# Two placements of exponentials on ScalarE in a hybrid decoder step: behind which high part of the weights they run

## The chip, the core and the metric

The kernel runs on one core of one Trainium2 chip. The metric is device time in microseconds (us) from start to end of one execution; the figure given for a kernel is the median of several runs. A profile is one further execution, recorded by the hardware profiler, with times in us from the start of its span.

The core's engines are TensorE (PE: matmuls; PEld: its weight loads), VectorE (DVE), ScalarE (ACT), GpSimd (POOL) and SyncE (SP, which here only issues DMAs). Each takes its instructions in the order that the program gave it.

## The reference

The reference is one inference step of a hybrid decoder layer, for 256 prompt tokens and 8 sample tokens (264 columns). One combined input projection gives queries, keys and values of a windowed attention, and z, x, B, C and dt of a state-space mixer. The mixer's scan over the prompt, which the change touches, works in two chunks of 128 tokens:

```python
la = jnp.cumsum(dt * a, axis=2)
seg = la[:, :, :, None] - la[:, :, None, :]
decay = jnp.exp(jnp.where(causal, seg, -jnp.inf))
cb = jnp.einsum('bclgn,bcsgn->bclsg', cm, bm)
y = jnp.einsum('bclsgh,bcsghp->bclghp', cb[..., None] * decay, xdt)
...
y = y + jnp.einsum('bclgn,bcghpn->bclghp', cm, h_prev) * jnp.exp(la)[..., None]
```

The exponential in `decay` is that of the differences inside a chunk; `jnp.exp(la)` in the last line is that of the decays by which the state carried from the chunk before enters the output. After the mixer come an output projection, a cross-attention over 256 memory tokens and a convolutional feed-forward block, all in float32.

## The kernel before

**Projections.** Every weight matrix is streamed from HBM in parts of 128 x 1024 floats (512 KB). `weights` (lines 76 to 92) loads a part into wraw (line 83, queue of SP, four buffers), ScalarE casts it to a high part whi (line 89), and VectorE subtracts to get the low part wlo (line 90); both have four buffers. The list `highs` collects the casts and `lows` the subtractions in the order in which the program writes them down. `proj` multiplies each part three times (high by high, high by low, low by high: lines 105 to 107), 264 columns at a time. In the input projection a pair of output blocks (256 columns) takes two units of two parts, so four parts: four casts, four subtractions, 96 matmuls. The pair's two sums lie in two PSUM banks; VectorE evacuates them, with the row factor r0, into u (line 789 for x, B and C; line 948 for z). The banks of the tag "mm" are three and of "t" two, so the second half of a pair can need a bank that the pair before has to give up.

**The mixer's order.** x comes in four groups of two pairs each (`conv_group`, lines 932 to 940: projection, causal convolution on ScalarE line 770 and VectorE line 772, tanh line 773, and the sample tokens' part with tsm, line 782), then z in eight pairs (`z_pair`, line 946 on; tanh line 953, squares 293 and 296, splits 98). The scan of group g (`ssd_prompt`, lines 832 to 897) is written down between them: group 0 behind the projections of conversion group 1, group 1 behind those of group 2, groups 2 and 3 behind the first and the second z pair.

**The scan of one group.** `logs` (line 820 on) loads the tile late with rows of la, broadcast over partitions: two blocks of 1024 columns, one per chunk (line 825), and 512 columns for the carried state (line 829, two DMAs). It is issued on SP's queue behind the last weight load written down by then, from the second call on. ScalarE then turns each chunk's block into decays: eight Relus that subtract la (line 847) and an exponential (line 848). VectorE multiplies by the masked product of B and C (line 849), TensorE multiplies by x (line 877). The 512 columns get one exponential (line 890); VectorE multiplies the carried state's output by it (line 891), and GpSimd adds it to x (line 892).

**What sets the order.** A planner in the compiler simulates the program and writes each engine's instructions in the order in which the simulation could start them, those marked with `high_priority` (all of `weights`) first. `tc.issue_after(ins)` adds one condition for the instructions in its block that run on ins's engine: they come behind ins there. Line 845 puts a chunk's Relus and exponential behind `highs[2 * c - 4]`: of the four casts of the last pair written down, the first for chunk 0 and the third for chunk 1. Line 890 has no such condition. Nearby there is also the attention of the sample tokens, whose matmuls (line 739) read zz, which VectorE fills (line 732) from a transposition (line 284), and the product of the sample tokens' states (lines 929 and 930).

Of the kernel before, what the change touches and what calls it, by code (L numbers as in the profile page):

```python
# [9 lines left out]
AF = mybir.ActivationFunctionType  # L10
# [38 lines left out]
def hybrid_decoder_step_kernel(ctx: ExitStack, tc: tile.TileContext, I, O):  # L49
    nc = tc.nc  # L50
    V, S, P, PE = nc.vector, nc.scalar, nc.gpsimd, nc.tensor
# [9 lines left out]
    def psum(tag):  # L61
        return ps.tile([128, 512], F32, tag=tag, name=tag, bufs=banks[tag])
# [39 lines left out]
    lows, highs = [], []  # L102
# [166 lines left out]
    def pc(name, i=0, n=1):  # L269
        o = _PC[name][0]  # L270
        return par[:, o + i:o + i + n]
# [10 lines left out]
    def tr(out, in_):  # L282
        k = in_.shape[0]
        return PE.transpose(out, in_, cst[0:k, C_ID:C_ID + k])  # L284
# [547 lines left out]
    def ssd_prompt(g):  # L832
        hs = slice(8 * g, 8 * g + 8)
        hp = mp.tile([128, 512], F32, tag="hp", name="hp", bufs=1)
        late = lates[g]
        p = psum("s")
        es, xdts = [], []
        for c in range(2):
            cs = slice(c * 128, c * 128 + 128)
            cbt = p[:, 256 * c:256 * c + 128]  # L840
            cbm = p[:, 256 * c + 128:256 * c + 256]
            PE.matmul(cbt, BT[:, g, cs], CT[:, g, cs], start=True, stop=True)
            V.tensor_tensor(out=cbm, in0=cbt, in1=tri, op=ALU.mult)
            e = late[:, 1024 * c:1024 * c + 1024].rearrange("p (h l) -> p h l", h=8)
            with tc.issue_after(highs[2 * c - 4].ins):
                for j in range(8):
                    S.activation(out=e[:, j, :], in_=e[:, j, :], func=AF.Relu, scale=-1.0, bias=la[:, c * 32 + 8 * g + j:c * 32 + 8 * g + j + 1])
                S.activation(out=e, in_=e, func=AF.Exp, scale=-1.0)
            V.tensor_tensor(out=e, in0=e, in1=cbm.unsqueeze(1).broadcast_to([128, 8, 128]), op=ALU.mult)
            es.append(e)  # L850
        sts = []
        for c in range(2):
            p = psum("x")
            for i in range(4):
                tr(p[:, i * 128:i * 128 + 128], xs[g][:, i, c * 128:c * 128 + 128])
            xdt = mp.tile([128, 8, 64], F32, tag="xdt", name="xdt", bufs=2)
            V.tensor_tensor(out=xdt, in0=p.rearrange("p (h q) -> p h q", h=8),
                            in1=dtn[:, c, hs].unsqueeze(2).broadcast_to([128, 8, 64]), op=ALU.mult)
            xdts.append(xdt)
            xw = mp.tile([128, 8, 64], F32, tag="bc", name="xw", bufs=2)  # L860
            V.tensor_tensor(out=xw, in0=p.rearrange("p (h q) -> p h q", h=8),
                            in1=de[:, c, hs].unsqueeze(2).broadcast_to([128, 8, 64]), op=ALU.mult)
            sts.append(xw)

        def state(c):
            st = psum("x")
            PE.matmul(st, Bn[:, c, g, :], sts[c].rearrange("p h q -> p (h q)"), start=True, stop=True)  # L867
            return st

        S.copy(out=hp, in_=state(0))  # L870
        for i in range(4):
            S.activation(out=xs[g][:, i, :TP], in_=xs[g][:, i, :TP], func=AF.Copy, scale=pc("d_skip", 4 * g + i))
        ys = [psum(k) for k in ("y", "s")]

        def own(c, h):
            o = (h % 2) * 64
            return PE.matmul(ys[c][o:o + 64, (h // 2) * 128:(h // 2) * 128 + 128], xdts[c][:, h, :], es[c][:, h, :], start=True, stop=True)

        with tc.issue_after(own(1, 7).ins):
            for c in range(2):  # L880
                for h in range(7 if c else 8):
                    own(c, h)
        for c in range(2):
            x = xs[g][:, :, c * 128:c * 128 + 128]
            V.tensor_tensor(out=x, in0=x, in1=ys[c].rearrange("p (i l) -> p i l", i=4), op=ALU.add)
        yi = psum("y")
        for i in range(4):
            PE.matmul(yi[:, i * 128:i * 128 + 128], hp[:, i * 128:i * 128 + 128], CT[:, g, 128:256], start=True, stop=True)
        ti = late[:, 2048:2560].rearrange("p (i l) -> p i l", i=4)
        S.activation(out=ti, in_=ti, func=AF.Exp)  # L890
        V.tensor_tensor(out=ti, in0=yi.rearrange("p (i l) -> p i l", i=4), in1=ti, op=ALU.mult)
        P.tensor_tensor(out=x, in0=x, in1=ti, op=ALU.add)
        st = state(1)
        hl = hp.rearrange("p (h q) -> p h q", h=8)
        P.tensor_tensor(out=hl, in0=hl, in1=d1[:, hs].unsqueeze(2).broadcast_to([128, 8, 64]), op=ALU.mult)
        V.tensor_tensor(out=hp, in0=hp, in1=st, op=ALU.add)
        nc.sync.dma_start(out=O["state_p"][g], in_=hp)
# [91 lines left out]
    with tc.issue_after(marks["load"].ins):  # L989
        logs()  # L990
    ssd_prompt(0)
    conv_group(2)
    with tc.issue_after(marks["load"].ins):
        logs()
    ssd_prompt(1)
    conv_group(3)
    with tc.issue_after(marks["load"].ins):
        logs()
    nc.sync.dma_start(out=O["conv_new"], in_=cnew)
    for i in range(8):  # L1000
        z_pair(i)
        ssd_sample(*([3, 1] if i in (1, 3, 5) else [1]))
        if i < 2:
            ssd_prompt(2 + i)
        if i in (3, 5, 7):
            res_load()
# [646 lines left out]
```

## Time and profile before

| | before |
|---|---|
| runs, us | 1385.97, 1385.55, 1385.59; median 1385.59 |
| profiled execution, us | 1385.11 |
| its span, us | 1383.3 |
| mean granted TensorE clock | 0.999 |
| DMA | 298.31 MB, mean 216 GB/s |

In a page of the profile a row of engines gives busy time, share of the span and instructions. In a list in order of time, a row has its start, its duration, engine, line and operation, what it writes and reads ("whi<-wraw"), shapes, and in square brackets the idle time of the engine before it with what ended it. In a list of waits, a row names who waited for whom, the total in us, how often, and the longest. A tile's view gives smallest, median and largest duration in ns and the starts of the first and the last instruction. The label "SPq" stands for DMAs issued on SP's queue. The profiler sees some of ScalarE's and VectorE's instructions overlap by about 0.1 us.

### The profile page before, as it was taken

The page shows a single profiled execution, that of the slowest core. Times are in us where ns is not written, and L with a number is a line of the kernel's source. Part 1 is how long each engine was busy: PE and PEld are TensorE (multiplying, and loading weights), DVE is VectorE, ACT ScalarE, POOL GpSimd, SP SyncE. Part 2 cuts the span into 40 slices and gives each one's busy share as a digit, 9 for nine tenths or more (in the row PEclk, how much of TensorE's full clock was granted, in tenths as well). Part 3 has the DMA queues.
Part 4 walks back from the last instruction along what each step waited for, and adds up shares of the span by engine and source line. Part 5 has one row for each costly group of instructions (what it writes and reads, how often), then busy time and mean ns, then how long its engine had stood idle before and what let it go on. Part 6 is the DMA issues. An engine that isn't in the chain of part 4 may idle for free.

```text
span 1383.3 us, 28658 instructions
## 1 busy us (share of the span) xinstructions
PE 1372.1 (99%) x11412; PEld 1348.4 (97%) x11412; DVE 1042.0 (75%) x1797; ACT 770.8 (56%) x1255; POOL 90.6 (7%) x284
## 2 busy tenths in 40 slices
PE   9999989999999999999999999999999999999998
PEld 8999989999999999899999999999999999999998
DVE  8879869999997784579777775776577657765655
ACT  7667666755545555566565544554455445543532
POOL 0000101111100000002010000000000000000000
PEclk9999999999999999999999999999999999999999
DMA  7954576766776566866576766676566655655654
GB/s 299 329 157 152 170 238 218 246 214 209 238 244 231 190 225 212 316 236 196 186 259 213 260 214 185 213 257 216 184 213 244 198 184 198 199 183 183 194 185 138
DMA packets 88325, 298.31 MB, mean 216 GB/s; under 512 B 11904, under 2 KB 17024, under 8 KB 87680
## 3 DMA queue, kind: packets, MB, share of 16 engines
q1 hardware_dynamic: 82688, 277.61, 60.2%
q0 software_dynamic: 5504, 18.88, 4.1%
q8 instruction: 89, 1.46, 0.4%
q14 instruction: 44, 0.36, 0.1%
HBM read 280.77 MB, written 16.23 MB: 215 GB/s over the span
## 4 chain that ended last, share of the span: by engine, by line
PE 95%; DMA 2%; DVE 1%; ACT 1%; issue 0%; SPq 0%; ACTq 0%
PE mm L106 20%; PE mm L105 20%; PE mm L107 20%; PE t L106 10%; PE t L107 9%; PE t L105 9%; DMA late<-dram_la 1%; PE t L246 1%; PE t L284 1%; PE x L867 0%; DMA wraw<-in_w_in_dram 0%; DVE wlo L90 0%; PE mm L246 0%; PE s L246 0%; DMA open<-in_open_dram 0%
## 5 line engine op out<-in xcount | busy, mean ns | idle before, releaser
L89 ACT CAST whi<-wraw 128x1024 fp32r<-128x1024 f32 x440 | 459.8, 1047 | 520.0 <-PE mm L106 270.1
L90 DVE TENSOR_TENSOR wlo<-wraw,whi 128x1024 fp32r<-128x1024 f32 x440 | 541.0, 1231 | 225.9 <-ACT whi L89 219.8
L106 PE MATMUL t<-x2l,whi 128*128 128x264 f32 x704 | 200.6, 285 | 0.0
L106 PE MATMUL mm<-hl,whi 128*128 128x264 f32 x704 | 199.6, 285 | 0.0
L107 PE MATMUL t<-x2h,wlo 128*128 128x264 f32 x704 | 199.1, 283 | 0.0
L107 PE MATMUL mm<-hh,wlo 128*128 128x264 f32 x704 | 197.6, 282 | 0.0
L105 PE MATMUL t<-x2h,whi 128*128 128x264 f32 x704 | 196.5, 279 | 0.0
L105 PE MATMUL mm<-hh,whi 128*128 128x264 f32 x704 | 194.1, 280 | 0.0
L106 PE MATMUL mm<-x2l,whi 128*128 128x264 f32 x672 | 191.5, 285 | 0.0
L107 PE MATMUL mm<-x2h,wlo 128*128 128x264 f32 x672 | 189.9, 283 | 0.0
L105 PE MATMUL mm<-x2h,whi 128*128 128x264 f32 x672 | 187.5, 279 | 0.0
L105 PE MATMUL mm<-xh,whi 128*128 128x264 f32 x576 | 165.6, 288 | 4.7 <-DVE u L789 4.7
L107 PE MATMUL mm<-xh,wlo 128*128 128x264 f32 x576 | 164.6, 287 | 0.0
L106 PE MATMUL mm<-xl,whi 128*128 128x264 f32 x576 | 164.5, 286 | 0.0
L105 PEld LDWEIGHTS t<-x2h,whi 128*128 128x128 f32 x704 | 132.3, 188 | 0.0
L107 PEld LDWEIGHTS t<-x2h,wlo 128*128 128x128 f32 x704 | 132.1, 188 | 0.0
L107 PEld LDWEIGHTS mm<-hh,wlo 128*128 128x128 f32 x704 | 131.9, 188 | 0.0
L106 PEld LDWEIGHTS mm<-hl,whi 128*128 128x128 f32 x704 | 131.7, 187 | 0.0
L106 PEld LDWEIGHTS t<-x2l,whi 128*128 128x128 f32 x704 | 131.7, 187 | 0.0
L105 PEld LDWEIGHTS mm<-hh,whi 128*128 128x128 f32 x704 | 131.2, 188 | 0.0
L105 PEld LDWEIGHTS mm<-x2h,whi 128*128 128x128 f32 x672 | 126.3, 188 | 0.0
L107 PEld LDWEIGHTS mm<-x2h,wlo 128*128 128x128 f32 x672 | 126.1, 188 | 0.0
(522 smaller groups left out, 2932.9 us busy)
## 6 DMA issues: line engine op xcount, KB each, us to landing
wraw<-in_w_up_dram SPq DMA_DIRECT2D x176, 512.0 KB, 4.2
wraw<-in_w_in_dram SPq DMA_DIRECT2D x96, 512.0 KB, 4.4
wraw<-in_w_dn_dram SPq DMA_DIRECT2D x88, 512.0 KB, 4.2
wraw<-in_w_out_dram SPq DMA_DIRECT2D x48, 512.0 KB, 4.6
h<-in_h_dram POOLq DMA_DIRECT2D x32, 256.0 KB, 4.3
hn<-in_h_dram SPq DMA_DIRECT2D x16, 512.0 KB, 4.7
out_state_s_dram<-hn POOLq DMA_DIRECT2D x16, 512.0 KB, 3.3
late<-dram_la SPq DMA_DIRECT2D x8, 512.0 KB, 7.1
```

The source lines that it names most:

```text
L89: highs.append(S.copy(out=hi, in_=x))
L90: lows.append(V.tensor_tensor(out=lo, in0=x, in1=hi.bitcast(F32), op=ALU.subtract))
L105: PE.matmul(out, wh, xh, start=start, stop=False)
L106: PE.matmul(out, wh, xl, start=False, stop=False)
L107: return PE.matmul(out, wl, xh, start=False, stop=stop)
L246: PE.matmul(first[c][:, :T], pre[k // 2][i][:, k % 2, c * 128:(c + 1) * 128], A[k // 8][x][:, k % 8, :], start=k + i + x == 0, stop=k == K ...
L284: return PE.transpose(out, in_, cst[0:k, C_ID:C_ID + k])
```

## The change

Two edits in `ssd_prompt`. The Relus and the exponential of chunk c are placed behind the second cast (chunk 0) and the fourth (chunk 1) of the last pair, in place of the first and the third. The exponential of line 890 gets a condition: behind the fourth cast of that pair.

```diff
-            with tc.issue_after(highs[2 * c - 4].ins):
+            with tc.issue_after(highs[2 * c - 3].ins):
                 for j in range(8):
                     S.activation(out=e[:, j, :], in_=e[:, j, :], func=AF.Relu, scale=-1.0, bias=la[:, c * 32 + 8 * g + j:c * 32 + 8 * g + j + 1])
                 S.activation(out=e, in_=e, func=AF.Exp, scale=-1.0)
...
         ti = late[:, 2048:2560].rearrange("p (i l) -> p i l", i=4)
-        S.activation(out=ti, in_=ti, func=AF.Exp)
+        with tc.issue_after(highs[-1].ins):
+            S.activation(out=ti, in_=ti, func=AF.Exp)
```

No instruction is added or removed; the planner orders the whole program anew with these conditions.

## The prediction

> **What bounds the kernel now.** I read the page first, then TensorE's waits in the stretch that the change touches, then ScalarE's order there, and last every engine around the longest wait.
>
> ```profile
> span 1383.3 us, 28658 instructions
> PE 1372.1 (99%) x11412; PEld 1348.4 (97%) x11412; DVE 1042.0 (75%) x1797; ACT 770.8 (56%) x1255; POOL 90.6 (7%) x284
> ```
>
> TensorE is busy for 1372.1 of 1383.3 us. So a change that takes no matmul away can only win what TensorE idles (11.2 us in all), and whatever it runs slowly for. The state-space mixer's ScalarE work lies between about 170 and 335 us. TensorE's waits there are these:
>
> ```profile
> PE mm L105 <- DVE u L789: 4.7, 1, 4.7
> PE s L739 <- DVE zz L732: 1.1, 1, 1.1
> PE x L867 <- ACT hp L870: 0.2, 1, 0.2
> ```
>
> Three waits, 6.0 us. The first is one event: the second projection pair of conversion group 1 (call it A; its four weight parts are A1 to A4) has not been evacuated into u, so the next pair (C, the first of group 2) has no PSUM bank for its second half. To see who is to blame I read ScalarE in order of time:
>
> ```profile
> 176.58 1.05 ACT L89 CAST whi<-wraw 128x1024 fp32r<-128x1024 f32 x1 [0.42 <-ACT own L726]
> 180.80 2.45 ACT L847 ACTIVATE late<-late,la 128x128 f32<-128x128 f32 x8 [3.17 <-DMA late<-dram_la]
> 183.16 0.21 ACT L782 ACTIVATE tsm<-csm 128x32 f32<-128x32 f32 x1
> 183.85 0.63 ACT L890 ACTIVATE late<-late 128x512 f32<-128x512 f32 x1 [0.48 <-DMA late<-dram_la]
> 184.39 1.03 ACT L89 CAST whi<-wraw 128x1024 fp32r<-128x1024 f32 x1
> ...
> 186.80 1.03 ACT L89 CAST whi<-wraw 128x1024 fp32r<-128x1024 f32 x1
> 187.74 2.44 ACT L847 ACTIVATE late<-late,la 128x128 f32<-128x128 f32 x8
> 190.09 1.03 ACT L89 CAST whi<-wraw 128x1024 fp32r<-128x1024 f32 x1
> ```
>
> The four casts are A1, A2, A3 and A4. The Relus of the first chunk stand behind A1 and those of the second behind A3, as line 845 asks. The exponential of the carried state (L890) has no such order and stands where its data were planned to be there. Both wait for the DMA that fills late, and everything behind them in ScalarE's queue waits too. What that costs in group 1 is next; the rows are of all engines:
>
> ```profile
> 201.73 0.28 PE L105 MATMUL mm<-xh,whi 128*128 128x264 f32 x1
> 201.85 0.28 PE L106 MATMUL mm<-xl,whi 128*128 128x264 f32 x1
> 203.64 0.63 ACT L890 ACTIVATE late<-late 128x512 f32<-128x512 f32 x1 [5.62 <-DMA late<-dram_la]
> 204.17 1.97 ACT L89 CAST whi<-wraw 128x1024 fp32r<-128x1024 f32 x2
> 205.23 1.23 DVE L90 TENSOR_TENSOR wlo<-wraw,whi 128x1024 fp32r<-128x1024 f32 x1 [5.26 <-ACT whi L89]
> 206.38 0.77 DVE L789 TENSOR_TENSOR u<-mm,r 128x264 f32<-128x264 f32 x2
> ...
> 206.85 0.59 PE L105 MATMUL mm<-xh,whi 128*128 128x264 f32 x1 [4.73 <-DVE u L789]
> ```
>
> This is one chain. L890 waits 5.62 us for its DMA; the casts C3 and C4 queue behind it; VectorE's subtraction for C3 waits 5.26 us for the cast; the evacuation u stands behind that subtraction; TensorE waits 4.73 us for u. The exponential's own result is needed only tens of microseconds later.
>
> **The change, part by part.**
>
> *The moved exponential.* It adds and removes no instruction; it puts L890 behind the fourth cast of the last projection pair that was written down before it. For group 1 that is the fourth cast of the second pair of group 2 (B4), long after C3, so the wait in front of C3 cannot stand there any more. TensorE's idle time there goes: 4.73 us. Who waits for the moved instruction? Only L891, and the slack is large:
>
> ```profile
> L848 ACT ACTIVATE late<-late x8: 1045/1056/1064, 185.3 to 278.2; 128x1024 f32<-128x1024 f32 x8
> L849 DVE TENSOR_TENSOR late<-late,s x8: 1202/1214/1219, 207.9 to 313.1; 128x1024 f32<-128x1024 f32 x8
> L890 ACT ACTIVATE late<-late x4: 629/632/633, 183.9 to 250.2; 128x512 f32<-128x512 f32 x4
> L891 DVE TENSOR_TENSOR late<-y,late x4: 677/691/696, 231.1 to 328.8; 128x512 f32<-128x512 f32 x4
> ```
>
> In group 0 the new place is behind A4 (190.09) and the use is at 231.1. In group 3 the last chunk's exponential L848 runs at 278.2 and the last L891 at 328.8; L890 now runs beside that L848. The cost of four instructions of 0.63 us is the same before and after, so I cost the move itself at nothing; what hides it is ScalarE's idle time (it is busy 56%).
>
> *The clock behind that wait.* After 4.73 us without a matmul TensorE did not come back at full speed, and the same window shows how full VectorE is afterwards:
>
> ```profile
> 170.00:335.00 165.00, 159.03 (x1372) 152.23 (x1372) 149.92 (x274) 103.56 (x191) 21.99 (x29) 0.99 0.71 224
> 207.00:210.20 3.20, 3.20 (x16) 3.20 (x17) 3.20 (x8) 1.41 (x3) 0.00 (x0) 0.54 0.55 164
> 210.20:335.00 124.80, 124.64 (x1057) 118.91 (x1057) 120.31 (x205) 80.41 (x148) 19.84 (x25) 1.00 0.69 221
> ```
>
> The columns are the length, then busy time of PE, PEld, DVE, ACT and POOL, the granted clock, the DMA share and GB/s. From 207.00 to 210.20 us the granted clock averages 0.54, so 0.46 x 3.20 = 1.47 us of work was lost. Without the wait this goes too.
>
> The Trainium skill (TensorE: Matmul & The Clock Gate, Part 1: The HAM clock gate) says that the half rate follows a window of about 3.4 us in which TensorE idled, and that these windows run freely, not from the start of the kernel. The trace agrees with half the rate and about the length. By that rule a 4.73 us gap holds a whole window in only (4.73 - 3.4) / 3.4 = 39% of the phases, so by the page's figure this term would be worth 0.6 us on average instead of 1.47.
>
> *The Relus behind A2 and A4 instead of A1 and A3.* Before, A2's cast stood behind the first Relu block, which waited 3.17 us for its DMA, and behind L890. One part is 24 matmuls at 0.12 us (201.73 to 201.85), 2.88 us, so A2 is due at about 176.58 + 2.88 = 179.5 us, and the Relus can follow at 180.8, when their data land: the wait shrinks to a few tenths and holds up no cast. What that held up, on VectorE and TensorE:
>
> ```profile
> 182.94 0.27 PE L284 MATMUL t<-cst,own 128*128 128x128 f32 x1
> 183.41 0.19 DVE L783 SCALAR_TENSOR_TENSOR ysam<-tsm,csm 128x32 f32<-128x32 f32 x1 [2.74 <-ACT tsm L782]
> 185.45 1.23 DVE L90 TENSOR_TENSOR wlo<-wraw,whi 128x1024 fp32r<-128x1024 f32 x1 [1.33 <-ACT whi L89]
> 187.20 0.28 DVE L732 COPY zz<-t 128x128 f32<-128x128 f32 x1
> 187.54 1.08 PE L739 MATMUL s<-vc,zz 128*32 128x128 f32 x32 [1.09 <-DVE zz L732]
> ```
>
> The copy zz had its input at 183.2 us and ran at 187.20, because VectorE had stood for 2.74 us for L782 (behind the Relus) and 1.33 us for A2. With A2's subtraction done by 182 or so, zz can run before TensorE arrives at 186.4: the 1.09 us go. The Relus themselves run one part later; the nearest reader, L849, follows its L848 by over 20 us (185.3 against 207.9 first, 278.2 against 313.1 last), so that costs nothing.
>
> *Queues.* No DMA belongs to the moved instructions, so nothing is issued at another place on SP's or POOL's queue; SP's weight loads can only come earlier, since they wait for VectorE's subtractions to release their buffers. The one new queueing is behind the fourth cast: eight Relus (2.44), L848 (1.06) and L890 (0.63), 4.13 us in a row, and the next pair's first cast and its subtraction wait behind them. The cover is the lead of the casts over TensorE, tightest in the crowded stretch where two groups' Relus come close together:
>
> ```profile
> 279.84 1.05 ACT L89 CAST whi<-wraw 128x1024 fp32r<-128x1024 f32 x1
> ...
> 283.06 1.23 DVE L90 TENSOR_TENSOR wlo<-wraw,whi 128x1024 fp32r<-128x1024 f32 x1
> ...
> 289.58 0.43 DVE L948 TENSOR_TENSOR u<-t,r 128x264 f32<-128x264 f32 x1
> ```
>
> The first cast of the third z pair at 279.84 is split by 284.3, and TensorE needs it only when the pair before ends, at about 289.5: a lead of 5.2 us against a burst of 4.13. I cost it at nothing, and price the loss of that cover as a rival.
>
> *Sum.* 4.73 + 1.47 + 1.09 = 7.29 us. The profiled execution took 1385.11 us (its span and 1.8 us around it) and gives 1377.8. The median of the runs shown, 1385.59, lies 0.48 us above; it gives 1378.3. I forecast 1378.2. A loss isn't excluded (the last rival prices it); the most that can be won is all three waits and the slow clock, 6.0 + 1.47 = 7.5, with a little over for restarts such as the 0.59 us matmul at 206.85.
>
> **The rivals.**
>
> *The slow clock was not in the timed runs.* Then only 4.73 + 1.09 = 5.82 us go, and the median falls to 1379.8. For it: the granted clock is known for one execution only. Against: the profiled one paid the 1.47 us and is still the fastest of the four times shown, which lie within 0.86 us (1385.11 to 1385.97), less than the term itself. The Trainium skill's rule on free-running windows (page and section as above) would bring this about. 0.10.
>
> *Something else is late at the same two places.* In group 1 the load of C3 is hidden behind L890's wait: it landed somewhere before 204.17, where the cast ran. If it landed at 200 us (an estimate between those ends), its cast, its subtraction (1.05 + 1.23) and u (0.4) let TensorE on at 202.8 instead of 201.97, a wait of about 0.9; and zz may stay where it is in VectorE's order and keep its 1.09. With one or both the gain is 5.3 to 6.4 and the time 1379.2 to 1380.3. For it: late's loads were in flight at the same time and took until 203.6. Against: VectorE releases the weight buffers earlier. 0.15.
>
> *VectorE is the bound behind TensorE.* From 210.2 to 335 us it is busy for 120.31 of 124.80 us, 96%. If it can't follow a TensorE that is 7 us ahead, the gain is given back as waits for u. Against: the three VectorE waits quoted (2.74, 1.33, 5.26) are 9.33 us that it gets back, more than the 7.29 needed, and TensorE waits for it nowhere after 207. If half of the 9.33 returns as other waits, 4.7 us are won (1380.9); if three quarters, 2.3 (1383.3); if all, nothing. 0.13, most of it at 1382.8 or above.
>
> *The burst starves the casts: slower.* Where the Relus, both exponentials and a z pair's own ScalarE work come between the fourth cast and the next pair's first one for longer than the 5.2 us lead, the cast is late, the subtraction is late, and u behind it: the chain of 203.64 again, priced as it was there at 4.73 + 1.47 = 6.2. It can strike in groups 2 and 3, whose Relus lie between 254 and 280 us. Twice 6.2 less the 7.29 won is 5.1 us slower, 1390.7. It decides once the casts' lead falls below the burst; the trace has 5.2 against 4.13, so against it, but not by much. 0.12.
>
> **How the numbers follow.** The forecast has 0.50: 1376.0 to 1379. Four cases make it faster; about 0.2% (2.8 us) is what a measurement of this kernel can tell from no change. Faster by more than that (below 1382.8): 0.50 + 0.10 + 0.15 and 0.04 of the VectorE case, 0.79. Within: the remaining 0.09. Slower: 0.12. The range goes from 1376.0 (everything, and the small restarts) up through the first two rivals into the VectorE case, 1384.0; it leaves out the slower case and the last of that one.
>
> **What would show it.** In the changed kernel's profile L890 should have no idle time before it in any group, and the wait of TensorE for u L789 should be gone, with a granted clock of 1.00 throughout 200 to 215 us. The waits of VectorE for a cast near 185 and 205 should be gone, and L739 should not wait for zz. The span should be near 1376. I am wrong if TensorE's wait returns at another evacuation, above all between 255 and 295 us behind a row of Relus, or if the casts of pair C now wait for their own DMA.

## The result and the profile after

| | before | after |
|---|---|---|
| median of the runs, us | 1385.78 (1385.55 to 1388.19, 6 runs) | 1377.12 (1376.67 to 1377.68, 6 runs) |
| profiled execution, us | 1385.11 | 1376.67 |
| its span, us | 1383.3 | 1374.9 |

The medians lie 8.66 us apart. The ratio over all the runs is 0.9933, with a 95% interval of 0.992 to 0.9946; it isn't the quotient of the medians, here or below. 1378.2 was forecast, with 1376.0 to 1384.0 as the range. In the changed kernel every line behind 890 has a number higher by one (the exponential is L891).

The page of the profile after, its engines:

```profile
span 1374.9 us, 28657 instructions
PE 1369.4 (100%) x11412; PEld 1346.3 (98%) x11412; DVE 1044.4 (76%) x1797; ACT 770.6 (56%) x1255; POOL 90.8 (7%) x284
```

TensorE idles for 1374.9 - 1369.4 = 5.5 us where it idled for 11.2. Its list of waits after:

```profile
PE x L207 <- DVE eps L280: 1.2, 1, 1.2
PE t L246 <- ACT xh L167: 0.5, 1, 0.5
```

Both lie ahead of the mixer; the waits for u, zz and hp are gone. ScalarE in order of time, after:

```profile
179.18 1.05 ACT L89 CAST whi<-wraw 128x1024 fp32r<-128x1024 f32 x1 [1.05 <-PE mm L106]
180.14 2.45 ACT L847 ACTIVATE late<-late,la 128x128 f32<-128x128 f32 x8
...
188.69 0.62 ACT L891 ACTIVATE late<-late 128x512 f32<-128x512 f32 x1
...
195.22 1.05 ACT L89 CAST whi<-wraw 128x1024 fp32r<-128x1024 f32 x1 [1.66 <-PE mm L106]
...
214.37 0.62 ACT L891 ACTIVATE late<-late 128x512 f32<-128x512 f32 x1
```

None of the four L891 has idle time before it. A2's cast (179.18) and C3's (195.22, at 204.17 before) now wait last for the matmuls that still read their buffer, and no longer behind an instruction that waits for a DMA. The windows of the prediction, after:

```profile
170.00:335.00 165.00, 165.00 (x1440) 158.79 (x1439) 159.53 (x282) 107.73 (x198) 23.08 (x31) 1.00 0.74 234
...
207.00:210.20 3.20, 3.20 (x29) 3.20 (x28) 3.20 (x6) 3.20 (x10) 0.00 (x0) 1.00 0.74 230
210.20:335.00 124.80, 124.80 (x1061) 119.27 (x1060) 121.78 (x203) 78.89 (x141) 20.39 (x26) 1.00 0.69 221
```

TensorE is busy in all of the 165 us and does 1440 matmuls there, against 1372. Where the time was won shows in three lines that both kernels have, the scores' matmuls ahead of the stage, the states' matmuls, and the last residual sums (first and last start are the numbers before the shape). Before:

```profile
L716 PE MATMUL s<-kcT,zz x32: 273/273/298, 172.1 to 172.9; 128*32 128x129 f32 x32
L867 PE MATMUL x<-xw,Bn x16: 590/592/697, 218.8 to 325.3; 128*128 128x512 f32 x16
L1480 DVE TENSOR_TENSOR res<-mm,res x96: 418/428/435, 808.8 to 1379.7; 128x264 f32<-128x264 f32 x96
```

and after:

```profile
L716 PE MATMUL s<-kcT,zz x32: 273/273/298, 171.8 to 172.6; 128*32 128x129 f32 x32
L867 PE MATMUL x<-xw,Bn x16: 590/592/697, 210.8 to 314.2; 128*128 128x512 f32 x16
L1481 DVE TENSOR_TENSOR res<-mm,res x96: 414/427/434, 800.4 to 1371.2; 128x264 f32<-128x264 f32 x96
```

The lead is 0.3 us at 172, 8.0 at the first L867 and 8.4 to 8.5 from 800 us to the end. All but those 0.3 us was won in the mixer, and nothing is given back later.

### The profile page after: what moved, and what is told of

It reads as the page before. It is cut to its first block, busy times and chain, and to the rows that moved or that the text cites. A ratio compares the mean times of both kernels' runs of the same rounds, so it can differ in the third digit from the quotient of the medians.

```text
span 1374.9 us, 28657 instructions
## 1 busy us (share of the span) xinstructions
PE 1369.4 (100%) x11412; PEld 1346.3 (98%) x11412; DVE 1044.4 (76%) x1797; ACT 770.6 (56%) x1255; POOL 90.8 (7%) x284
## 4 chain that ended last, share of the span: by engine, by line
PE 99%; DMA 0%; ACT 0%; SPq 0%; DVE 0%; issue 0%
PE mm L105 21%; PE mm L107 21%; PE mm L106 21%; PE t L107 10%; PE t L105 10%; PE t L106 10%; PE t L246 1%; PE t L284 1%; PE x L867 1%; PE mm L246 0%; PE s L246 0%; PE x L284 0%; PE t L569 0%; DMA open<-in_open_dram 0%; PE s L877 0%; PE y L877 0%
## 5 line engine op out<-in xcount | busy, mean ns | idle before, releaser
L106 PEld LDWEIGHTS mm<-x2l,whi 128*128 128x128 f32 x672 | 125.9, 187 | 0.0
```

Of the source, the lines that this page charges most:

```text
L106: PE.matmul(out, wh, xl, start=False, stop=False)
```

## The experiments

My theory was that the exponential's wait, by its place in ScalarE's queue, held up C3's cast, VectorE's queue behind that cast's subtraction, and TensorE; the Relus' move was to add the 1.09 us of zz. The rivals were that the exponential does it all, that what stands behind it is late anyway, and that any hole of that length on ScalarE costs as much. In each set of experiments the kernel before ran on the same chip. Its median was 1385.7 beside the two halves, group 1 and the three other groups, 1385.42 beside group 0, the experiment with u and the convolution and the other execution of before, and 1385.18 beside the rest. Ratios are to these runs. Each profile is of one execution.

**One half alone.** The exponential's condition without the Relus' move:

```diff
-        S.activation(out=ti, in_=ti, func=AF.Exp)
+        with tc.issue_after(highs[-1].ins):
+            S.activation(out=ti, in_=ti, func=AF.Exp)
```

> Only the exponential of line 890 is placed behind the fourth cast; the Relus keep their old places. My account (the 4.73 us wait for u and the slow clock belong to the exponential, the 1.09 us wait for zz to the Relus): the wait for u and the half clock are gone, the wait for zz stays between 0.6 and 1.1 us, and the time is 1385.6 - 6.2 to 6.6, so 1379.0 to 1379.4. Rival (the exponential alone does all of it, the Relus' move nothing): 1377, with no wait for zz. Rival (it takes both, because the planner orders all anew): the wait for u stays, 1384 or above.

Measured: 1376.95 (5 runs), 0.9938 [0.9926, 0.995], all of the change's gain: the time of the first rival, not my 1379.0 to 1379.4. TensorE's list of waits has one row, L207 ahead of the mixer. ScalarE's order in this kernel:

```profile
178.61 2.45 ACT L847 ACTIVATE late<-late,la 128x128 f32<-128x128 f32 x8 [0.95 <-DMA late<-dram_la]
...
181.08 1.04 ACT L89 CAST whi<-wraw 128x1024 fp32r<-128x1024 f32 x1
```

A2's cast (181.08) still stands behind the first Relus, which wait 0.95 us, and that is early enough: the wait for zz, which I had given to the Relus, is gone without their move. Two things brought A2 forward by 3.3 us here: the exponential is out of its way (its wait and its work were 0.48 + 0.63 us), and the first chunk's rows landed earlier, so that the Relus start at 178.61 in place of 180.80. That second part varies from execution to execution (see group 0 below). zz runs 3.4 us behind A2's cast in this kernel (184.50). With the landing of the first profile of before, A2 would be cast at about 183.3 and zz at 186.7, and TensorE would still wait some 0.6 us (an estimate from these rows). So this trace doesn't show that the Relus' place never matters; the medians show no difference.

The Relus' move without the exponential's condition:

```diff
-            with tc.issue_after(highs[2 * c - 4].ins):
+            with tc.issue_after(highs[2 * c - 3].ins):
```

> Only the Relus are moved, behind the second and fourth cast; the exponential has no condition. My account: group 1's exponential still stands before C3 and waits over 4 us for its DMA, TensorE still waits 4 to 5 us for u and then runs at half the clock; at most the wait for zz goes, 1384.5 to 1385.6. In group 0 the exponential may now hold up A2 itself, since no Relu has waited before it. Rival (the Relus do the main part): below 1381.

Measured: 1386.79 (11 runs), 1.0007 [0.9998, 1.0015], nothing won, and above my 1384.5 to 1385.6. TensorE's list of waits, of this kernel:

```profile
PE mm L105 <- DVE u L789: 4.5, 1, 4.5
PE x L867 <- ACT hp L870: 1.8, 1, 1.8
...
PE s L739 <- DVE zz L732: 1.7, 1, 1.7
```

and ScalarE's order in it:

```profile
183.32 0.63 ACT L890 ACTIVATE late<-late 128x512 f32<-128x512 f32 x1 [4.82 <-DMA late<-dram_la]
183.86 1.03 ACT L89 CAST whi<-wraw 128x1024 fp32r<-128x1024 f32 x1
184.80 2.45 ACT L847 ACTIVATE late<-late,la 128x128 f32<-128x128 f32 x8
```

The Relus moved out of the way of A2, and the planner put the exponential into the place that came free. It waits 4.82 us there, and A2's cast waits with it as before, only for another instruction.

**Which group's exponential.** The condition for group 1 only, then for the three others only (in both, an else branch issues the exponential without it):

```diff
+        if g == 1:
+            with tc.issue_after(highs[-1].ins):
...
```

> Only group 1's exponential gets the condition; those of groups 0, 2 and 3 stay, and so do the Relus. My account: this one instruction carries the wait for u and the slow clock, so the time is that of moving all four, within 0.5 us: 1379.0 to 1379.6; groups 2 and 3 still show ScalarE waiting 2.7 and 3.9 us for DMAs that cost TensorE nothing. Rival (the four waits of 12.7 us together use up ScalarE's lead, so that each is worth a share): 1382 or above.

Measured: 1380.11 (1377.01 to 1385.38, 8 runs), 0.996 [0.9945, 0.9975]. Group 1 was to bring nearly everything; it brings 5.6 us, in a wide scatter, a time between my account's and the rival's. TensorE's waits in the profiled execution (1382.79), and then ScalarE's order in it (L894 is the unconditioned exponential):

```profile
PE x L867 <- ACT hp L870: 3.2, 2, 2.2
PE s L739 <- DVE zz L732: 1.9, 1, 1.9
```

```profile
247.88 0.63 ACT L894 ACTIVATE late<-late 128x512 f32<-128x512 f32 x1 [5.97 <-DMA late<-dram_la]
...
248.53 0.57 ACT L870 COPY hp<-x 128x512 f32<-128x512 f32 x1
```

u's wait is gone. But behind the exponential of the last group stands hp, the copy of the carried state that the next matmuls of L867 wait for (2.2 us), and zz is still late.

```diff
+        if g != 1:
+            with tc.issue_after(highs[-1].ins):
...
```

> The reverse: groups 0, 2 and 3 get the condition, group 1 doesn't; Relus unchanged. My account: the wait of about 5 us before C3 stays and with it 4 to 5 us of TensorE's wait and the half clock, 1385.0 to 1385.7. Rival (each of the four waits has a share): 1383 or below.

Measured: 1383.17 (1381.02 to 1385.54, 11 runs), 0.9982 [0.9974, 0.9991]: 2.5 us, 0.2 above what the rival said and well below my 1385.0. Waits of TensorE, profiled execution (1382.38), and two windows of it:

```profile
PE mm L105 <- DVE u L789: 3.4, 1, 3.4
```

```profile
200.00:204.30 4.30, 0.94 (x8) 0.73 (x7) 1.62 (x3) 2.52 (x4) 0.00 (x0) 1.00 0.41 148
204.30:208.50 4.20, 4.19 (x23) 4.19 (x24) 4.20 (x9) 3.23 (x8) 0.00 (x0) 0.62 0.44 129
```

zz and hp are gone, u stays. 5.6 and 2.5 us are 8.1 of 8.66: the groups' shares nearly add up, and the four are one effect at several places.

Group 0 alone tells whose the 2.5 us are:

```diff
-        S.activation(out=ti, in_=ti, func=AF.Exp)
+        with tc.issue_after(highs[-1].ins) if g == 0 else ExitStack(): S.activation(out=ti, in_=ti, func=AF.Exp)
```

> Only group 0's exponential gets the condition. Theory A (a wait of ScalarE in group 0 makes the one in group 1 longer, since late subtractions release the weight buffers late and so put off SP's loads, those of late among them): the loads of group 1's rows go out 2 to 3 us earlier than at 190.6, the wait for u shrinks from 4.7 to 3 to 3.7 us, the wait for zz is gone, and the time is that of moving groups 0, 2 and 3, 1382.5 to 1384. Theory B (groups 2 and 3 give the 2.5 us): 1385 or above.

Measured: 1382.37 (1381.06 to 1388.01, 10 runs), 0.9979 [0.9965, 0.9993], about 3 us: group 0's alone does what the three did together, within the scatter. That is theory A, a little outside its figures. Its profile has no wait for zz, and u's is 3.8:

```profile
PE mm L105 <- DVE u L789: 3.8, 1, 3.8
```

How group 0 reaches group 1 shows on SP's queue, where group 1's rows are issued, before and then in this kernel:

```profile
190.60 0.89 SPq L825 DMA_DIRECT2D late<-dram_la  x2
```

```profile
187.25 0.80 SPq L825 DMA_DIRECT2D late<-dram_la  x2
```

Both are 6.2 us behind A2's cast (184.39 and 181.05). In the other traces with the Relus and the loads in their old places it is 5.9 to 6.6. A late A2 means late subtractions, the weight loads wait for those to free their buffers (13.7 us of SP's queue from 170 to 215 us, before), and the rows stand behind them. So a wait in group 0 puts off group 1's rows.

A2 itself is late for two reasons, and zz with it. The exponential costs it 1.1 to 1.8 us (its wait and its work, in the five traces that have it and the Relus where they were). The landing of the first chunk's rows does the rest, and it moves from execution to execution: the Relus start between 178.57 and 181.47 us, though the loads go out between 172.8 and 173.5. In the last experiment on VectorE the exponential stands where it was, but the rows land early, and TensorE doesn't wait for zz either:

```profile
178.63 2.46 ACT L847 ACTIVATE late<-late,la 128x128 f32<-128x128 f32 x8 [0.85 <-DMA late<-dram_la]
...
182.89 1.03 ACT L89 CAST whi<-wraw 128x1024 fp32r<-128x1024 f32 x1
```

So the 1.09 us were not the exponential's alone.

**The place of the wait, and its length.** In the next two the planner orders everything anew around another placement. First the kernel before, with the loads of the carried state's rows issued ahead of the chunks':

```diff
-        for c in range(2):
-            nc.sync.dma_start(out=w[:, 1024 * c:1024 * c + 1024].rearrange("p (h l) -> p h l", h=8),
-                              in_=dram_la[c, 8 * g:8 * g + 8, :].partition_broadcast(128))
...
+        for c in range(2):
+            nc.sync.dma_start(out=w[:, 1024 * c:1024 * c + 1024].rearrange("p (h l) -> p h l", h=8),
+                              in_=dram_la[c, 8 * g:8 * g + 8, :].partition_broadcast(128))
```

> The kernel before, but the rows for the carried state (line 829) are loaded before the two chunks' blocks (line 825), so their data land earlier; the exponential has no condition. My account: the fault is that the planner puts the exponential where it believes the data to have landed, so it now puts it earlier too, and ScalarE waits before another cast: total waits of line 890 of 5 us or more stay, some of it still reaches TensorE, 1380 to 1385. Rival (only the DMA's lateness was at fault): the exponential's waits vanish and the time is 1378.5 to 1379.5.

Measured: 1379.57 (1377.93 to 1379.72, 5 runs), 0.9953 [0.9942, 0.9965]. The time lies between the two forecasts; what decides is the waits, of which over 5 us were to stay. The planner moved the exponentials forward with the loads, and they still wait:

```profile
178.84 0.63 ACT L890 ACTIVATE late<-late 128x512 f32<-128x512 f32 x1 [3.00 <-DMA late<-dram_la]
179.38 1.04 ACT L89 CAST whi<-wraw 128x1024 fp32r<-128x1024 f32 x1
...
195.80 0.63 ACT L890 ACTIVATE late<-late 128x512 f32<-128x512 f32 x1 [3.10 <-DMA late<-dram_la]
```

In all they wait 11.6 us, 12.7 before, and TensorE waits 0.5 for u and 0.2 for zz in the place of 4.7 and 1.1, in the profiled execution (1378.14); the median lies 2.4 us above the changed kernel's. So with both orders of the loads the planner puts the exponential ahead of the landing; the times that it assumes stand in no run. And the cost is not in proportion to the wait: holes of 3 us ahead of A1 and C2 are nearly covered, those of 5 to 6 us ahead of C3 are not. Place and length changed together here.

Then the changed kernel, with 18 copies of 128 columns (with no reader; ScalarE is busy for 776.2 us in place of 770.6) ahead of C3's cast:

```diff
+def planned_block(tc, S, marks, behind):
+    with tc.issue_after(behind.ins):
+        for _ in range(18):
+            last = S.activation(out=marks["blk"], in_=marks["blk"], func=AF.Copy)
+    return last
...
-                highs.append(S.copy(out=hi, in_=x))
+                with tc.issue_after(blk(highs).ins) if len(highs) == 50 else ExitStack(): highs.append(S.copy(out=hi, in_=x))
```

> The changed kernel with 18 copies of a 128-column scratch tile put on ScalarE between the casts C2 and C3, about 5.5 us of work that the planner knows of (the scratch result is used nowhere). Account A (a hole of that length is harmful only because VectorE's order was made without it, with the subtraction ahead of u): TensorE waits under 1 us, 1377 to 1378. Account B (the casts' lead is too short for any hole of 5.5 us there): TensorE waits about 4.7 us again and then has the half clock, 1382 to 1383.5.

Measured: 1377.05 (5 runs), 0.994 [0.9928, 0.9952]. TensorE waits for nothing in the mixer, though C3's cast starts only at 201.23. First ScalarE, then VectorE of this kernel, in order of time:

```profile
199.66 1.67 ACT L1659 ACTIVATE blk<-blk 128x128 f32<-128x128 f32 x5
201.23 2.94 ACT L89 CAST whi<-wraw 128x1024 fp32r<-128x1024 f32 x3
```

```profile
197.18 0.43 DVE L789 TENSOR_TENSOR u<-mm,r 128x264 f32<-128x264 f32 x1 [0.35 <-PE mm L107]
...
198.69 0.42 DVE L789 TENSOR_TENSOR u<-mm,r 128x264 f32<-128x264 f32 x1
...
200.22 0.68 DVE L861 TENSOR_TENSOR xw<-x,de 128x512 f32<-128x512 f32 x1
...
202.93 1.22 DVE L90 TENSOR_TENSOR wlo<-wraw,whi 128x1024 fp32r<-128x1024 f32 x1
```

A hole of this length that the planner knows of costs nothing: it writes u, and the product xw that TensorE needs next, ahead of C3's subtraction. That fits account A: the price in the kernel before was that of an order made for a C3 that was on time. But C3 is cast 2.9 us earlier here than in the kernel before (204.17), so the two holes are not equally late, and the next two experiments change VectorE's order in the kernel before itself.

**The link on VectorE.** If u's place behind C3's subtraction is what TensorE waits for, putting u first should win the time without moving the exponential. The kernel before, with that one subtraction ordered behind pair A's u:

```diff
-                lows.append(V.tensor_tensor(out=lo, in0=x, in1=hi.bitcast(F32), op=ALU.subtract))
+                with tc.issue_after(marks["u"].ins) if len(lows) == 50 else ExitStack(): lows.append(V.tensor_tensor(out=lo, in0=x, in1=hi.bitcast(F32), op=ALU.subtract))
...
-        in_pair(lambda m, pm: V.tensor_tensor(out=us[:, m, 3:], in0=pm, in1=r0, op=ALU.mult))
+        in_pair(lambda m, pm: marks.update(u=V.tensor_tensor(out=us[:, m, 3:], in0=pm, in1=r0, op=ALU.mult)))
```

> The kernel before, with one order on VectorE: the subtraction for C3 stands behind the evacuation u of pair A. The exponential still waits before C3. My account (u stuck behind the subtraction is the link): ScalarE still idles about 5 us before line 890, TensorE no longer waits for u and at most 1 us for the cast or subtraction of C3, the clock stays full: 1379 to 1380.5. Rival (TensorE needs C3 itself by then): it waits about as long for C3 instead, 1384 or above.

Measured: 1384.8 (1382.6 to 1387.58, 12 runs), 0.9996 [0.9987, 1.0006], no change. The time is the rival's, but TensorE waits neither for u, as I had said, nor for C3:

```profile
PE x L284 <- DVE xw L861: 3.9, 1, 3.9
PE x L867 <- ACT hp L870: 1.8, 1, 1.8
```

It waits for xw, the product that gives up a bank for the transpositions. VectorE in order of time:

```profile
199.60 0.43 DVE L789 TENSOR_TENSOR u<-mm,r 128x264 f32<-128x264 f32 x1
205.63 0.48 DVE L772 SCALAR_TENSOR_TENSOR c<-u,par,c 128x256 f32<-128x256 f32 x1 [5.60 <-ACT c L770]
206.04 0.42 DVE L789 TENSOR_TENSOR u<-mm,r 128x264 f32<-128x264 f32 x1
206.38 1.22 DVE L90 TENSOR_TENSOR wlo<-wraw,whi 128x1024 fp32r<-128x1024 f32 x1
```

Between the two halves of u the planner put a convolution step, whose input is ScalarE's L770, and that stands behind the waiting exponential as well (here 5.92 us, at 203.53). The second half of u, the subtraction and xw (at 208.78) all come behind it. So the last experiment moves that step too (pair A's convolution, behind u):

```diff
...
-        conv_side(b0, us, dst)
+        with tc.issue_after(marks["u"].ins) if b0 == 6 else ExitStack(): conv_side(b0, us, dst)
```

> The kernel before with VectorE's order changed further: both evacuations u of pair A stand ahead of its convolution and of the subtraction for C3, so nothing between them waits for ScalarE. Theory A (u is the only link to TensorE): no wait for u, nothing else above 1 us near 205 us, 1379 to 1380.5. Theory B (VectorE's whole queue is the link): TensorE waits 2 to 4 us for the next thing behind C3's subtraction, the product xw of line 861 that gives up the bank of the transpositions, 1382 to 1385.

Measured: 1381.65 (1380.03 to 1389.69, 10 runs), 0.998 [0.9964, 0.9996]: 3.8 us in the median, in a wide scatter. That is theory B's mechanism, with a wait and a time a little below its figures. The exponential still waits 4.96 us (at 201.50), TensorE no longer for u, but for this:

```profile
PE x L284 <- DVE xw L861: 1.7, 1, 1.7
...
PE x L867 <- ACT hp L870: 1.2, 1, 1.2
```

The last link is therefore VectorE's queue as a whole, not u: with u out of it, in both experiments, the next item that TensorE needs is late, the product xw.

**The burst.** The rival that forecast a slower kernel had casts starved behind a row of ScalarE work. The changed kernel with both chunks' Relus behind the last high part, so that all sixteen Relus of a group come there:

```diff
-            with tc.issue_after(highs[2 * c - 4].ins):
+            with tc.issue_after(highs[-1].ins):
```

> The changed kernel with the Relus of both chunks behind the fourth cast, so that about 7.6 us of ScalarE work stands behind it in place of 4.1. By the rival of the prediction the burst starves the casts once it is longer than their lead of about 5.2 us: then TensorE waits 2 to 5 us in groups 2 and 3, 1380 to 1389. If the planner lets the next casts pass the Relus, or the lead is longer than I read, no wait: 1377 to 1378.

Measured: 1376.77 (5 runs), 0.9938 [0.9926, 0.9949], as fast as the change, and TensorE waits for nothing in the mixer. The run of ScalarE work is there, in group 2 for example:

```profile
253.97 4.79 ACT L847 ACTIVATE late<-late,la 128x128 f32<-128x128 f32 x16
...
261.11 1.04 ACT L89 CAST whi<-wraw 128x1024 fp32r<-128x1024 f32 x1
```

From the first Relu to the next cast lie 7.3, 7.3, 7.1 and 5.2 us of ScalarE work in the four groups (some of it not the scan's; one or both chunk exponentials come only behind the next cast). In three of them this is longer than the lead of 5.2 us that I had read, at another place of the stretch. These runs don't tell whether the lead there was longer or the planned order covered it.

**Another execution of the kernel before**, to see whether the slow clock is the same each time:

> The kernel before once more, for the trace of another execution. In most of its executions the mean granted clock is 0.997, in the one that the prediction was read from 0.999. Theory A (the slow clock behind the wait for u lasts two windows in most executions instead of one, which is the 1.4 us that the sum lacks): a stretch at half clock of about 6.8 us behind 200 us, with TensorE's waits the same within 1 us. Theory B (the executions differ in how late the data of late land, and the waits of TensorE are longer): half clock as before, about 3.4 us, but waits of 7 us or more in all.

Measured: 1385.19 (8 runs), 0.9998 [0.9987, 1.0009]; the profiled execution took 1384.16, with a wait for u of 4.1 us and for zz of 0.7. Its windows around u's wait:

```profile
201.30:205.50 4.20, 0.15 (x2) 0.00 (x0) 1.58 (x3) 2.51 (x3) 0.00 (x0) 0.77 0.46 181
205.50:210.50 5.00, 4.95 (x22) 4.96 (x23) 5.00 (x10) 3.18 (x7) 0.00 (x0) 0.51 0.38 108
```

A shorter wait, and yet 0.49 x 5.0 = 2.4 us of work lost to the clock, against 1.47 in the execution that I had read. Theory A holds: in windows of half a microsecond the clock is 1.00 up to 203.5, 0.60 up to 204.0, 0.50 up to 210.0, 0.57 up to 210.5 and 1.00 behind it, so about 6.8 us at half rate (203.6 to 210.4, worked out from these means), where the first execution had about 3.4 (206.5 to 209.9); the waits are 0.6 and 0.4 us shorter. Theory B's 7 us of waits are not there (4.8).

**Does it add up?** Each profiled time, less TensorE's waits in the mixer, less what the lower clock cost (one less the granted clock, times the window behind the longest wait), should give the same floor:

| kernel | time | waits | clock | rest |
|---|---|---|---|---|
| before | 1385.11 | 6.0 | 1.47 | 1377.6 |
| before, again | 1384.16 | 4.8 | 2.4 | 1377.0 |
| Relus only | 1387.57 | 8.3 | 1.7 | 1377.6 |
| exponential, group 1 | 1382.79 | 5.1 | 0 | 1377.7 |
| exponential, others | 1382.38 | 3.4 | 1.6 | 1377.4 |
| exponential, group 0 | 1383.0 | 3.8 | 2.6 | 1376.6 |
| rows first | 1378.14 | 0.7 | 0 | 1377.4 |
| u first | 1385.66 | 6.3 | 1.7 | 1377.7 |
| u and convolution first | 1380.8 | 2.9 | 0 | 1377.9 |
| after | 1376.67 | 0 | 0 | 1376.7 |

It does, within 1.3 us, where the times differ by 10.9. So these two terms explain the differences down to about 1 us, and with no wait left in the mixer nothing more can be won there by taking waits away: the exponential alone, the planned block, the burst and the change lie between 1376.8 and 1377.1, closer than their runs scatter.

## Why the prediction was right

- *The moved exponential, 4.73 us.* Right, in size and mechanism. The wait for u went with group 1's condition (the others alone leave 3.4 to 3.8 us of it), a planned hole of about its length costs nothing, and the two experiments on VectorE show the chain's last link. That link was drawn too narrowly: not u alone, but whatever TensorE needs behind the held subtraction.
- *The move costs nothing, hidden by ScalarE's idle time.* Right: busy time 770.6 against 770.8, no reader waits. The loads issued on SP's queue came earlier, as I said they could.
- *The clock, 1.47 us.* The mechanism was right, and the size was that of one execution. It is 1.47 in one profile of before and 2.4 in the other. Of 67 further executions of before, 11 had a mean granted clock of 0.999, with a median of 1384.32, 10 had 0.998 and 46 less, and the 45 of these at 0.997 had a median of 1385.51. The one whose profile I read has 0.999. So the rival that the timed runs were free of the slow clock had it the wrong way round: most seem to pay more than the profiled one. Only the mean clock of those runs is known, and it counts slow time inside the pause too.
- *The Relus' move removes zz's 1.09 us.* A2 was cast at 179.18 (179.5 was predicted) and the Relus followed at 180.14 without a wait, but the step that gave them zz's wait failed, though its 1.09 us were won. The exponential alone wins them, the Relus alone don't. I had read the 3.17 us in front of the first Relus as what held A2 up and left the exponential behind them out. Without it A2 is cast at 181.08 even behind the Relus; with it, and the Relus moved, A2 waits until 183.86. How late the rows land is the other part, and it differs between executions by up to 2.9 us; the sum took one execution's. The Relus' new place is worth nothing that these medians can tell (1376.95 without it, 1377.12 with it).
- *Groups 0, 2 and 3.* I gave group 0 nothing but its place, and the later groups nothing. Group 0 is worth about 3 us in the median. Part of that reaches TensorE through group 1, whose rows go out earlier. A later group's exponential cost hp 0.2 us in the profile that I read, but 2.2 us in another kernel's, with the copy behind it.
- *The sum, 7.29 us.* Between the two profiled executions 8.44 were won. About 0.3 lie ahead of the stage, and 0.2 are hp's wait, which the sum left out. The rest is TensorE's busy time in the mixer: 159.03 us from 170 to 335 before (1372 matmuls), 157.00 us from 170 to 327 after (1373), so 2.0 us where the sum had the clock's 1.47. The 0.59 us matmul right behind u's wait, which the prediction named as a little over, is of that kind. In the medians the larger clock loss is in it too.
- *VectorE as the bound.* It fell. VectorE is busy for 121.78 of 124.80 us after 210.2, 98%, and TensorE waits for it nowhere: a queue can be nearly full and still in time.
- *The burst.* It fell: runs of 5.2 to 7.3 us behind the fourth cast held up nothing.
- *Something else late at the same places.* C3's load was there: its cast waits for TensorE to release the buffer, not for a DMA. With group 1's condition alone C4's cast did wait 4.15 us for its load, and u still did not wait.

## What to carry to other kernels

When an instruction with a late reader waits for a DMA on an in-order engine, look not at its reader but at what stands behind it, and follow that queue by queue to the engine that sets the end; it is best placed behind the work that is wanted first. Price such a wait by what the last engine waits, not by its own length: in one profile 11.6 us of it in short holes cost 0.7 us, in another one hole of 5.6 us cost 4.7 and the clock behind it. And try each half of a two-part change alone: here one half did all that the medians show, and the other only looked useful beside it.

## What the runs showed of the hardware

A TensorE that paused for less than 4 us came back at half rate in several kernels, and pauses of 1.7 to 2.2 us did not have this. The shortest pause that did was 3.4 us (the exponential for the other groups: granted clock 0.62 over the 4.20 us behind it), and 4.1 us in the second execution of before cost more than 4.73 in the first. In the second execution the clock fell inside the pause already (0.77 from 201.3 to 205.5), some 2.1 us after TensorE stopped, and stayed at 0.51 for the next 5 us. With group 0's exponential alone it fell 2.2 us into the pause, too (at 202.5), and with the others' only 1.0 us after the pause (at 205.3). The slow stretch lasted about 3.4 us (in the first execution and with the others' exponentials) or about 6.8 (in the second and with group 0's alone). Over the 3.4 us ahead of the fall, TensorE still worked for 1.0 to 1.3 us in these three traces (worked out from these times), so it need not idle for as long as a slow stretch lasts. How much work would keep the clock up, no run here shows. The Trainium skill (TensorE: Matmul & The Clock Gate, Part 1: The HAM clock gate) speaks of free-running windows of about 3.4 us. That the phase varies agrees with these runs; my estimate from the page, that only 39% of the executions would pay, does not: none of the 67 had a mean granted clock of 1.0 and 56 had 0.998 or less, where the 21 executions of the four kernels without a wait in the mixer (the exponential alone, the planned block, the burst, the change) had 1.0 in 19 cases and 0.999 in two.
